# Down projection: the last three wide matmuls of one stretch alternate with the first four narrow ones of the next, at two places

## The chip, the cores and the metric

One core of a Trainium2 chip runs the whole program in one launch. The metric is device time in microseconds (us). The kernel before took 2168.19 us as the median of three runs (2166.08 to 2170.76). Engines go by these names: PE (TensorE, matmuls) with its weight loads PEld, DVE (VectorE), ACT (ScalarE), POOL (GpSimd) and SP (SyncE, which only issues DMAs here).

## What is computed

One decoder block, float32, 512 tokens, model width 2048: modulated RMS norm, a combined input projection, two token mixers, an output projection, and then the gated MLP on which this case turns:

```python
D_MODEL = 2048; SEQ = 512; D_FF = ((8 * D_MODEL // 3 + 255) // 256) * 256     # 5632 = 44 * 128

def _conv_ffn(h, w_up, conv_w, conv_b, w_down):
    u = h @ w_up                                   # (512, 2 * 5632)
    y = conv_b + causal depthwise conv of width 3 over u
    val, gate = jnp.split(y, 2, axis=-1)
    return (jax.nn.silu(gate) * val) @ w_down      # (512, 5632) @ (5632, 2048)

x = x + gt2 * _conv_ffn(...)
return _rmsnorm(x, norm_f_g)
```

## The kernel before

Activations lie transposed: 128 features on the partitions, the 512 tokens along the free dimension. Each float32 product is made of three matmuls of rounded halves: the weight tile is split into a high part `wh` and a rest `wl`, the activation into `xh` and `xl`, and `mm3` (L131) issues `wh*xh`, `wh*xl` and `wl*xh` (L133, L134, L135) into one PSUM bank. ACT makes the high part (L1373) and DVE the rest (L1374), both in `wsplit`, into one of three rotating buffers that the profile names `uw`. So a 128x128 weight tile costs three matmuls, each with a weight load of its own. A matmul streams either all 512 tokens (here called wide) or a half of 256 (narrow).

The down projection has 44 blocks of 128 input features and 16 output tiles `f`, and is done in this order on PE:

1. `plain(A1, 0)`: 4 input blocks against all 16 output tiles, wide. Each tile's partial sum is copied out by ACT (L1675) and written to DRAM (`yd`, L1676) by POOL's queue. The profile names its operands `act`.
2. `strassen`: 16 input blocks by a scheme of seven products for eight over the two halves of tokens, of output tiles and of inputs. Eight rounds of seven products, 24 narrow matmuls each; the operands are named `Y` and `T`. Results are added to `yd` in DRAM by POOL's queue (L1688, L1731). In the last round `rest_pair` loads the activations of the remaining blocks (L1500).
3. `down_four` and the loop over `f` up to 7: the 20 remaining blocks (`A3`), wide, 60 matmuls for a tile. `load_x2` fetches the residual `x2` and the stored `yd` of a tile (POOL's queue, L1821) and adds them (DVE, L1822); `last_residual` adds the tile's PSUM (DVE, L1250), sums squares for the norm (ACT L1241, DVE L1242) and scales. `gate_row` (DVE, L1789) works out the gates beside it.
4. `down_half(0, f)` for `f` = 8 to 15: the same for the first half of the tokens, narrow, 60 matmuls for a tile; then the same for the second half, and the final norm.

The order of each engine's instructions is set by a scheduling layer that simulates the program; `tc.issue_after` ties an instruction behind another. Small tiles of 512 columns (`Slot`) come from a list of about ten homes in strict rotation: `yd` in `load_x2` takes one, and so does `sqx` in `last_residual`; a new user waits until the last user of that home is done. DVE, ACT and the queues work in order.

Of the kernel before, what the change touches and what calls it, by code (L numbers as in the profile page):

```python
# [17 lines left out]
T = 512  # L18
D = 2048
KT = D // P  # L20
# [6 lines left out]
NWF = 8  # L27
# [40 lines left out]
def block_kernel(ctx, tc, a, out, stop=None, dbg=None):  # L68
    nc = tc.nc
    V, S, G, PE = nc.vector, nc.scalar, nc.gpsimd, nc.tensor  # L70
# [26 lines left out]
    def col(name, i):  # L97
        return vec[:, COLS[name] + i : COLS[name] + i + 1]
# [29 lines left out]
        eng.tensor_tensor(lo, raw, hi[:, :].bitcast(F32), op=ALU.subtract)  # L128
        return hi, lo

    def mm3(ps, wh, wl, xh, xl, start, stop, more=False):  # L131

        PE.matmul(ps, wh, xh, start=start, stop=False, skip_group_check=more)  # L133
        PE.matmul(ps, wh, xl, start=False, stop=False, skip_group_check=more)  # L134
        return PE.matmul(ps, wl, xh, start=False, stop=stop, skip_group_check=more)  # L135

    def project(ps, src, acts, start=True, stop=True, engs=(V,)):

# [50 lines left out]
    blocks = []  # L189
# [1005 lines left out]
    def bank():  # L1195
        return psm.tile([P, T], F32, tag="b", name="b")

    def half(acts, hf):
        sl = slice(hf * HT, (hf + 1) * HT)
        return [t[:, :, sl] for t in acts]  # L1200
# [5 lines left out]
    def wide(name):  # L1206

        return rb.tile([P, 4, HT], F32, tag="wide", name=name, bufs=3)
# [8 lines left out]
    def x2(f, sl=slice(0, T)):  # L1217
        return x2q[f // 4][:, f % 4, sl]
# [27 lines left out]
    def residual(f, pss, gate, acc, lo, hi, fresh):  # L1246

        x = x2(f, slice(lo, hi))
        for ps in pss:
            V.scalar_tensor_tensor(x, ps, gate, x, op0=ALU.mult, op1=ALU.add)  # L1250
        sumsq(acc, x, lo, hi, fresh)
# [115 lines left out]
    def wsplit(src, off=0):  # L1367
        n = src.shape[-1]
        i = nsplit[0] % 3
        nsplit[0] += 1  # L1370
        w = (ea, ea, ub)[i].tile([P, WS], F32R, tag=f"w{i}", name="uw")
        hi, lo = w[:, off : off + n], w[:, 2 * QW + off : 2 * QW + off + n]
        S.copy(hi, src)  # L1373
        lo_of[0] = V.tensor_tensor(lo, src, hi.bitcast(F32), op=ALU.subtract)  # L1374
        return hi, lo

    def product(ps, w, Y, start=True):
        wh, wl = wsplit(w, 16)
        n = w.shape[-1] // P
        for k in range(n):  # L1380
            sl = slice(k * P, (k + 1) * P)
            y = Y[k // 4]
            mm3(ps, wh[:, sl], wl[:, sl], y[:, 0, k % 4, :], y[:, 1, k % 4, :], start=start and k == 0,
                stop=k == n - 1, more=not start)
# [95 lines left out]
    NR = NF - 3 * ND  # L1480
# [84 lines left out]
    def last_operands(name):  # L1565
        for h in held:
            if h[0] != name:
                continue
            if len(h) == 4:
                make(name, h[1], pairwise(h[2]), 2, h[3])  # L1570
                h[2].done()
            else:
                make(*h)

    A1, A3 = [], []
# [9 lines left out]
    def last_product(p):  # L1585

        j, u1, u2, b, w22, x = p
        product(b, w22, T4, start=False)
        if x is None:
            S.copy(u2[:, H0], b)  # L1590
        else:
            V.tensor_add(u2[:, H0], x[:, H0], b)
            x.done()
        finish_pair(j, u1, u2)
# [64 lines left out]
    yd = [tc.dram_tile([P, T], F32, name=f"yd{f}") for f in range(KT)]  # L1659

    def plain(acts, k0):

        nk = len(acts)
        for f in range(KT):
            w = wide("wd").rearrange("p a b -> p (a b)")
            nc.sync.dma_start(w, a["wdn"][f, :, k0 * P : (k0 + nk) * P])
            wh, wl = wsplit(w, 0)
            ps = bank()
            for k in range(nk):
                sl = slice(k * P, (k + 1) * P)  # L1670
                mm3(ps, wh[:, sl], wl[:, sl], acts[k][:, 0, :], acts[k][:, 1, :], start=k == 0, stop=k == nk - 1)
            if f == 0:
                last_product(pend)
            s_ = Slot("yd")
            S.copy(s_.t, ps)  # L1675
            G.dma_start(yd[f], s_.t)  # L1676
            s_.done()
            for _ in range(2 if f else 1):
                next(prep, None)
        for _ in prep:  # L1680
            pass

    def last_down(p):

        f, u2, b, w22 = p
        product(b, w22, ops["T4"], start=False)
        S.activation(u2[:, H0], b, AF.Copy, scale=-1.0)
        G.dma_start(yd[f], u2.t, accum_op=ALU.add)  # L1688
        u2.done()

    def strassen(hook):

        wq = [rb.tile([P, 4 * QW], F32, tag=f"x2_{i}", name="wd4") for i in (0, 2, 1, 3)]
        pend = None
        for f in range(NWF):
            wa, wb = wq[2 * (f % 2)], wq[2 * (f % 2) + 1]
            w11, w12, w21, w22 = (t[:, s_] for t in (wa, wb) for s_ in (W1, W2))
            nc.sync.dma_start(wa, a["wdn"][f, :, ND * P : 3 * ND * P])
            nc.sync.dma_start(wb, a["wdn"][f + NWF, :, ND * P : 3 * ND * P])
            pa = bank()[:, 0:HT]  # L1700
            cap = Slot("cap")
            product(pa, w11, ops["Y11"])
            S.copy(cap[:, H0], pa)
            if pend:
                last_down(pend)
            u1 = Slot("u1")
            pb = bank()[:, 0:HT]
            product(pb, w12, ops["Y21"])
            V.tensor_add(u1[:, H0], cap[:, H0], pb)
            hook(f, 0)  # L1710
            u2 = Slot("u2")
            pc = bank()[:, 0:HT]
            r1 = wide("r1").rearrange("p a b -> p (a b)")
            V.tensor_add(r1, w21, w22)
            product(pc, r1, ops["T1"])
            S.copy(cap[:, H1], pc)
            if f == 0:
                last_operands("T3")
            hook(f, 1)
            r2 = wide("r2").rearrange("p a b -> p (a b)")  # L1720
            V.tensor_add(r2, r1, w11)
            product(pa, r2, ops["T2"], start=False)
            S.copy(cap[:, H0], pa)
            if f == 0:
                last_operands("T4")
            hook(f, 2)
            r4 = wide("r4").rearrange("p a b -> p (a b)")
            V.tensor_add(r4, r2, w12)
            product(pc, r4, ops["Y22"], start=False)
            V.tensor_add(u1[:, H1], cap[:, H0], pc)  # L1730
            G.dma_start(yd[f], u1.t, accum_op=ALU.add)  # L1731
            u1.done()
            hook(f, 3)
            r3 = wide("r3").rearrange("p a b -> p (a b)")
            V.tensor_add(r3, w11, w21)
            product(pa, r3, ops["T3"], start=False)
            V.scalar_tensor_tensor(u2[:, H1], pa, -1.0, cap[:, H1], op0=ALU.mult, op1=ALU.subtract)
            cap.done()
            pend = (f + NWF, u2, pa, w22)
        return pend  # L1740
# [5 lines left out]
    def in_last(f, i):  # L1746
        if f == NWF - 1:
            rest_pair(G)

    plain(A1, 0)  # L1750
    pend = strassen(in_last)

    wd2 = ea.tile([P, 2, 2 * QW], F32, tag="t41", name="wd2")
# [2 lines left out]
    def down_row():  # L1756
        if nrow[0] % 5 > 2:
            w = wd2[:, nrow[0] % 5 - 3, :]
        else:
            w = wide("wd").rearrange("p a b -> p (a b)")  # L1760
        nrow[0] += 1
        return w

    def down(ps, f, acts, blocks=(0, 8, 16)):
        for k0 in blocks:
            n = min(8, NR - k0)
            w = down_row()
            nc.sync.dma_start(w[:, 0 : n * P], a["wdn"][f, :, (3 * ND + k0) * P : (3 * ND + k0 + n) * P])
            wh, wl = wsplit(w[:, 0 : n * P], 16 if acts[0].shape[-1] == HT else 0)
            for k in range(n):  # L1770
                sl = slice(k * P, (k + 1) * P)
                x = acts[k0 + k]
                mm3(ps, wh[:, sl], wl[:, sl], x[:, 0, :], x[:, 1, :], start=k0 + k == 0, stop=k0 + k == NR - 1)

    cb = []

# [36 lines left out]
    def gate(f):  # L1813
        return mod[:, 80 + f : 81 + f]
# [12 lines left out]
    def down_half(hf, f):  # L1827
        ps = bank()[:, 0:HT]
        down(ps, f, half(A3, hf))
        last_residual(f, [ps], hf * HT, (hf + 1) * HT)  # L1830

    def last_residual(f, ps, lo, hi):
        residual(f, ps, gate(f), acc, lo, hi, f == 0)
        S.activation(x2(f, slice(lo, hi)), x2(f, slice(lo, hi)), AF.Identity, bias=eps[:, 2:3], scale=col("nf", f))
# [6 lines left out]
    for f in range(NWF):  # L1841
        if f == 0:
            pss = down_four()
        if f >= 4:
            gate_row()
        load_x2(f)
        ps = pss[f] if f < 4 else bank()
        if f >= 4:
            down(ps, f, A3)
            gate_row()  # L1850
        last_residual(f, [ps], 0, T)
    for f in range(NWF, KT):
        if gated[0] < KT and f % 2 == 0:
            gate_row()
# [111 lines left out]
```

## Time and profile before

| | us |
|---|---|
| median of the three runs | 2168.19 |
| the profiled execution's own time | 2164.5 |
| its span, first to last instruction | 2162.7 |
| DVE busy | 1677.9 |
| ACT busy | 1046.7 |
| POOL busy | 236.2 |
| down projection, from the first wide `act` matmul to the end | 1668 to 2163 |

The mean granted PE clock was 0.991. Section 1 of the page gives busy time as a share of the span, section 4 the chain of work that ended last. The timeline view has a row for each instruction with start, duration, engine, line, operands and shape; in square brackets stands the idle time before it and who ended that. PE's durations overlap, since matmuls are pipelined: the pace of PE is read from the starts, or from the number of matmuls in a stretch (the windows view, "x1106").

### The profile page before, as it was taken

What the parts mean: (1) busy time and instruction counts of PE and PEld (TensorE: products, weight loads), DVE (VectorE), ACT (ScalarE), POOL (GpSimd) and SP (SyncE); (2) the same over time, 40 slices, a digit from 0 to 9 for tenths busy, and PEclk for the clock granted to TensorE, in tenths of its full rate; (3) what the DMA queues carried; (4) which work ended last, traced back from release to release, by engine and by line L of the source; (5) the groups of instructions that cost most, each with busy time, mean ns of one, the idle gap of its engine ahead of it and who ended that gap; (6) DMA issues with size and microseconds to landing.
All of it is one profiled execution on the core that took longest, in us unless ns stands there. A gap on an engine that the chain in (4) does not pass through costs nothing.

```text
span 2162.7 us, 44015 instructions
## 1 busy us (share of the span) xinstructions
PE 2118.8 (98%) x17864; PEld 1874.0 (87%) x17864; DVE 1677.9 (78%) x2615; ACT 1046.7 (48%) x1510; POOL 236.2 (11%) x376
## 2 busy tenths in 40 slices
PE   8999999999999999999999999999999999999997
PEld 3567777777767889999999999999999899987897
DVE  7988898888854677888888877887778557768664
ACT  4354444443433466655555555555556444443353
POOL 0002122222100111101100100000000000120000
PEclk9999999999999999999999999999999999999998
DMA  9966665656437565988989877777777535598754
GB/s 393 405 220 197 199 203 170 204 172 185 145 111 269 184 197 186 289 252 250 244 250 260 223 212 209 209 207 206 207 211 226 196 124 138 143 334 307 240 184 165
DMA packets 169485, 471.89 MB, mean 218 GB/s; under 512 B 21361, under 2 KB 29505, under 8 KB 159169
## 3 DMA queue, kind: packets, MB, share of 16 engines
q1 hardware_dynamic: 120370, 352.12, 47.8%
q0 software_dynamic: 27696, 79.20, 17.5%
q10 hardware_dynamic: 21216, 37.76, 5.7%
q8 instruction: 140, 2.29, 0.4%
q14 instruction: 63, 0.52, 0.1%
HBM read 432.81 MB, written 36.18 MB: 217 GB/s over the span
## 4 chain that ended last, share of the span: by engine, by line
PE 87%; DMA 4%; DVE 4%; ACT 2%; issue 2%; POOL 0%; DVEq 0%; SPq 0%; ACTq 0%; POOLq 0%
PE b L135 19%; PE b L133 19%; PE b L134 19%; PE mm L631 11%; PE pf L412 4%; PE b L1203 2%; PE b L1204 1%; DMA wrow<-wup 1%; PE pb L1033 1%; DVE war L750 1%; DMA wraw<-wout 1%; DMA wa<-ada 1%; PE pa L697 0%; ACT x L1303 0%; PE pf L133 0%
## 5 line engine op out<-in xcount | busy, mean ns | idle before, releaser
L135 PE MATMUL b<-t,uw 128*128 128x256 f32 x1408 | 388.6, 276 | 0.0
L133 PE MATMUL b<-t,uw 128*128 128x256 f32 x1408 | 388.6, 276 | 0.0
L134 PE MATMUL b<-t,uw 128*128 128x256 f32 x1408 | 388.6, 276 | 0.0
L133 PE MATMUL b<-y,uw 128*128 128x256 f32 x1056 | 293.7, 278 | 2.9 <-ACT uw L1373 2.9
L135 PE MATMUL b<-y,uw 128*128 128x256 f32 x1056 | 292.9, 278 | 0.8 <-DVE uw L1374 0.7
L134 PE MATMUL b<-y,uw 128*128 128x256 f32 x1056 | 292.9, 277 | 0.0
L631 PE MATMUL mm<-ahl,whi 128*128 128x512 f32 x864 | 290.5, 410 | 2.0 <-DVE rk L534 1.4
L133 PEld LDWEIGHTS b<-t,uw 128*128 128x128 f32 x1408 | 264.3, 188 | 0.0
L134 PEld LDWEIGHTS b<-t,uw 128*128 128x128 f32 x1408 | 264.3, 188 | 0.0
L135 PEld LDWEIGHTS b<-t,uw 128*128 128x128 f32 x1408 | 264.3, 188 | 0.0
L1374 DVE TENSOR_TENSOR uw<-r,uw 128x1024 fp32r<-128x1024 f32 x164 | 200.4, 1223 | 79.1 <-ACT uw L1373 79.1
L1374 DVE TENSOR_TENSOR uw<-wquart,uw 128x1024 fp32r<-128x1024 f32 x156 | 190.7, 1223 | 68.0 <-ACT uw L1373 67.7
L1373 ACT CAST uw<-wquart 128x1024 fp32r<-128x1024 f32 x156 | 164.0, 1052 | 89.1 <-PE b L135 66.1
L1374 DVE TENSOR_TENSOR uw<-wd,uw 128x1024 fp32r<-128x1024 f32 (+1 forms) x112 | 123.9, 1108 | 105.6 <-ACT uw L1373 105.3
L135 PE MATMUL b<-act,uw 128*128 128x256 f32 (+1 forms) x608 | 202.2, 333 | 2.6 <-DVE uw L1374 2.6
L133 PEld LDWEIGHTS b<-y,uw 128*128 128x128 f32 x1056 | 199.7, 189 | 3.6 <-ACT uw L1373 3.5
L133 PE MATMUL b<-act,uw 128*128 128x256 f32 (+1 forms) x608 | 202.3, 333 | 0.0
L1373 ACT CAST uw<-r 128x1024 fp32r<-128x1024 f32 x164 | 172.5, 1052 | 61.5 <-PE b L135 61.5
L134 PE MATMUL b<-act,uw 128*128 128x256 f32 (+1 forms) x608 | 202.1, 332 | 0.0
L135 PEld LDWEIGHTS b<-y,uw 128*128 128x128 f32 x1056 | 199.7, 189 | 1.2 <-DVE uw L1374 1.2
L134 PEld LDWEIGHTS b<-y,uw 128*128 128x128 f32 x1056 | 199.7, 189 | 0.1
L631 PEld LDWEIGHTS mm<-ahl,whi 128*128 128x128 f32 x864 | 158.6, 189 | 43.3 <-issue 12.2
(356 smaller groups left out, 4600.9 us busy)
## 6 DMA issues: line engine op xcount, KB each, us to landing
wquart<-wup SPq DMA_DIRECT2D x176, 512.0 KB, 5.3
wa<-ada SPq DMA_DIRECT2D x48, 1024.0 KB, 9.5
war<-ada SPq DMA_DIRECT2D x192, 256.0 KB, 4.0
wd<-wdn SPq DMA_DIRECT2D x64, 512.0 KB, 4.4
wraw<-win ACTq DMA_DIRECT2D x118, 256.0 KB, 4.2
wraw<-wout SPq DMA_DIRECT2D x96, 256.0 KB, 3.5
wquart<-wup POOLq DMA_DIRECT2D x44, 512.0 KB, 6.8
r<-wup SPq DMA_DIRECT2D x44, 512.0 KB, 4.6
```

The source lines that it names most:

```text
L133: PE.matmul(ps, wh, xh, start=start, stop=False, skip_group_check=more)
L134: PE.matmul(ps, wh, xl, start=False, stop=False, skip_group_check=more)
L135: return PE.matmul(ps, wl, xh, start=False, stop=stop, skip_group_check=more)
L412: PE.matmul(pf[n % 2 * 4 + ii], w[:, sl], full[k], start=k == 0, stop=k == KT - 1)
L631: PE.matmul(ps, w[:, sl], x, start=first, stop=k == KT - 1 and i == 2)
L750: V.scalar_tensor_tensor(wa, wa, 1.0, cqs[kq], op0=ALU.mult, op1=ALU.mult, accum_out=modq[:, kq, j : j + 1])
L1033: PE.matmul(pt[HS[e], h, c * 2 * L : (c + 1) * 2 * L], nt[HS[e], s, :], rw[HS[e], s, :, :], start=True, stop=True)
L1203: PE.matmul(ps[:, :].rearrange("p (a b) -> p a b", a=2), wh, x, start=start, stop=False)
L1204: PE.matmul(ps[:, 0:HT], wl, x[:, 0, :], start=False, stop=stop)
L1373: S.copy(hi, src)
L1374: lo_of[0] = V.tensor_tensor(lo, src, hi.bitcast(F32), op=ALU.subtract)
```

## The change

Place 1 is the passage from `plain` to `strassen`, place 2 the passage from tile 7 to `down_half(0, 8)`. There `mm3` holds back the last three wide matmuls (`hold`), and the next call of `mm3`, which is the first of the narrow ones, issues its own first matmul, then one held back, its second, one held back, its third, and the last held back; the fourth narrow one follows. No matmul is added or taken away. What comes after the held sum moves behind the first narrow tile's code: `stored(15, ps)` (the copy of the last `plain` tile) behind the first product of `strassen`, `last_residual(7, ...)` behind the matmuls of `down_half(0, 8)`.

```diff
+    late = []
+    def mm3(ps, wh, wl, xh, xl, start, stop, more=False, hold=False):
+        muls = [lambda: PE.matmul(ps, wh, xh, ...), lambda: PE.matmul(ps, wh, xl, ...), lambda: PE.matmul(ps, wl, xh, ...)]
+        if hold:
+            late.extend(muls)
+            return None
+        if late:
+            ins = muls[0]()
+            for m in (late.pop(0), muls[1], late.pop(0), muls[2], late.pop(0)):
+                with tc.issue_after(ins.ins):
+                    ins = m()
+            return ins
...
@@ plain
-                mm3(ps, wh[:, sl], wl[:, sl], acts[k][:, 0, :], acts[k][:, 1, :], start=k == 0, stop=k == nk - 1)
+                mm3(ps, wh[:, sl], wl[:, sl], acts[k][:, 0, :], acts[k][:, 1, :], start=k == 0, stop=k == nk - 1,
+                    hold=f == KT - 1 and k == nk - 1)
...
+        return lambda: stored(KT - 1, ps)
@@ strassen
             product(pa, w11, ops["Y11"])
+            if f == 0:
+                finish_plain()
@@ down_half
         down(ps, f, half(A3, hf))
+        if f == NWF and hf == 0:
+            last_residual(NWF - 1, [held_ps], 0, T)
         last_residual(f, [ps], hf * HT, (hf + 1) * HT)
@@ the loop over wide tiles
-            down(ps, f, A3)
+            down(ps, f, A3, hold=f == NWF - 1)
...
-        last_residual(f, [ps], 0, T)
+        if f < NWF - 1:
+            last_residual(f, [ps], 0, T)
+    held_ps = ps
```

PE at place 1, before: the last wide matmuls of `plain` (operand `act_19145`) and the first narrow ones of `strassen` (`Y_19323`).

```order
L133 MATMUL b<-act_19145,uw 128x512
L134 MATMUL b<-act_19145,uw 128x512
L135 MATMUL b<-act_19145,uw 128x512
L133 MATMUL b<-Y_19323,uw 128x256
L134 MATMUL b<-Y_19323,uw 128x256
L135 MATMUL b<-Y_19323,uw 128x256
L133 MATMUL b<-Y_19323,uw 128x256
```

The same place in the changed kernel (its L135, L136 and L137 are the three matmuls of `mm3`):

```order
L135 MATMUL b<-Y_19323,uw 128x256
L135 MATMUL b<-act_19145,uw 128x512
L136 MATMUL b<-Y_19323,uw 128x256
L136 MATMUL b<-act_19145,uw 128x512
L137 MATMUL b<-Y_19323,uw 128x256
L137 MATMUL b<-act_19145,uw 128x512
L135 MATMUL b<-Y_19323,uw 128x256
```

Each of the last three wide matmuls now has a narrow one on either side; the rows ahead and behind are as they were. Place 2 is changed in the same way.

POOL's queue near place 2, before: the loads of `yd` for `load_x2` of tiles 7 to 15.

```order
L1821 DMA yd_22278<-yd7_19189 128x512
L1821 DMA yd_22370<-yd8_19190 128x512
L1821 DMA yd_22454<-yd9_19191 128x512
L1821 DMA yd_22539<-yd10_19192 128x512
L1821 DMA yd_22624<-yd11_19193 128x512
L1821 DMA yd_22709<-yd12_19194 128x512
L1821 DMA yd_22793<-yd13_19195 128x512
L1821 DMA yd_22877<-yd14_19196 128x512
L1821 DMA yd_22960<-yd15_19197 128x512
```

And in the changed kernel:

```order
L1844 DMA yd_22278<-yd7_19189 128x512
L1844 DMA yd_22454<-yd9_19191 128x512
L1844 DMA yd_22362<-yd8_19190 128x512
L1844 DMA yd_22539<-yd10_19192 128x512
L1844 DMA yd_22624<-yd11_19193 128x512
L1844 DMA yd_22709<-yd12_19194 128x512
L1844 DMA yd_22877<-yd14_19196 128x512
L1844 DMA yd_22960<-yd15_19197 128x512
L1844 DMA yd_22793<-yd13_19195 128x512
```

The load for tile 13 went from before 14 and 15 to behind them, since the rotation of the `Slot` homes is shifted by one: it now takes the home that `sqx` of tile 7 had, and waits for DVE's add of that tile (`acc`, before L1242); before, it took the home of `yd` of tile 8.

DVE at the same place, before: from the add of `yd` of tile 13 (L1822) to the weight rest of the second block of tile 9 (`uw_22488`).

```order
L1822 SCALAR_TENSOR_TENSOR x2_21565<-yd_22793,mod_87,x2_21565 128x512
L1374 TENSOR_TENSOR uw_22404<-wd_22402,uw_22404 128x1024
L1250 SCALAR_TENSOR_TENSOR x2_21563<-b_22281,mod_87,x2_21563 128x512
L1374 TENSOR_TENSOR uw_22433<-wd_22431,uw_22433 128x512
L1242 TENSOR_TENSOR acc_21566<-acc_21566,sqx_22361 128x512
L1374 TENSOR_TENSOR uw_22460<-wd_22458,uw_22460 128x1024
L1374 TENSOR_TENSOR uw_22488<-wd2_21561,uw_22488 128x1024
```

And in the changed kernel:

```order
L1388 TENSOR_TENSOR uw_22399<-wd_22397,uw_22399 128x1024
L1264 SCALAR_TENSOR_TENSOR x2_21563<-b_22281,mod_87,x2_21563 128x512
L1388 TENSOR_TENSOR uw_22428<-wd_22426,uw_22428 128x512
L1256 TENSOR_TENSOR acc_21566<-acc_21566,sqx_22444 128x512
L1388 TENSOR_TENSOR uw_22460<-wd_22458,uw_22460 128x1024
L1845 SCALAR_TENSOR_TENSOR x2_21565<-yd_22793,mod_87,x2_21565 128x512
L1388 TENSOR_TENSOR uw_22488<-wd2_21561,uw_22488 128x1024
```

The add of `yd` of tile 13 now stands five rows later, between two weight rests of tile 9, behind the `acc` of tile 7 that its load waits for.

More of the change, by code (lines that the diff above doesn't have):

```diff
@@ L129, in split_weights @@
         return hi, lo
[L131 to L135, printed above, removed]
+    late = []
+    def mm3(ps, wh, wl, xh, xl, start, stop, more=False, hold=False):
+        muls = [lambda: PE.matmul(ps, wh, xh, start=start, stop=False, skip_group_check=more),
+                lambda: PE.matmul(ps, wh, xl, start=False, stop=False, skip_group_check=more),
+                lambda: PE.matmul(ps, wl, xh, start=False, stop=stop, skip_group_check=more)]
+        if hold:
[7 more added lines that the diff above has]
+            return ins
+        for m in muls:
+            ins = m()
+        return ins
     def project(ps, src, acts, start=True, stop=True, engs=(V,)):
@@ L1670, in plain @@
                 sl = slice(k * P, (k + 1) * P)
-                mm3(ps, wh[:, sl], wl[:, sl], acts[k][:, 0, :], acts[k][:, 1, :], start=k == 0, stop=k == nk - 1)
+                mm3(ps, wh[:, sl], wl[:, sl], acts[k][:, 0, :], acts[k][:, 1, :], start=k == 0, stop=k == nk - 1,
+                    hold=f == KT - 1 and k == nk - 1)
             if f == 0:
                 last_product(pend)
[L1674 to L1677, printed above, removed]
+            if f < KT - 1:
+                stored(f, ps)
             for _ in range(2 if f else 1):
@@ L1681, in plain, with stored @@
             pass
+        return lambda: stored(KT - 1, ps)
+    def stored(f, ps):
+        s_ = Slot("yd")
+        S.copy(s_.t, ps)
+        G.dma_start(yd[f], s_.t)
+        s_.done()
     def last_down(p):
@@ L1748, in in_last @@
             rest_pair(G)
-    plain(A1, 0)
+    finish_plain = plain(A1, 0)
     pend = strassen(in_last)
@@ L1762, in down_row, with down @@
         return w
-    def down(ps, f, acts, blocks=(0, 8, 16)):
+    def down(ps, f, acts, blocks=(0, 8, 16), hold=False):
         for k0 in blocks:
@@ L1772, in down @@
                 x = acts[k0 + k]
-                mm3(ps, wh[:, sl], wl[:, sl], x[:, 0, :], x[:, 1, :], start=k0 + k == 0, stop=k0 + k == NR - 1)
+                mm3(ps, wh[:, sl], wl[:, sl], x[:, 0, :], x[:, 1, :], start=k0 + k == 0, stop=k0 + k == NR - 1,
+                    hold=hold and k0 + k == NR - 1)
     cb = []
```

## The prediction

> **What bounds the kernel now.** I read the page first, section 1 and the chain:
>
> ```profile
> PE 2118.8 (98%) x17864; PEld 1874.0 (87%) x17864; DVE 1677.9 (78%) x2615; ACT 1046.7 (48%) x1510; POOL 236.2 (11%) x376
> PE 87%; DMA 4%; DVE 4%; ACT 2%; issue 2%; POOL 0%; DVEq 0%; SPq 0%; ACTq 0%; POOLq 0%
> ```
>
> PE is always busy and makes up the chain. No work is removed, so only PE's pace can give anything, and a matmul's duration does not show pace. So next the number of matmuls in stretches where PE runs one kind without a gap (the windows view: stretch, length, PE's busy time and number, granted clock, DMA share and rate):
>
> ```profile
> 900.00:1660.00 760.00, 760.00 (x6709) 1.00 0.82 226
> 1760.00:1890.00 130.00, 130.00 (x1106) 1.00 0.54 154
> 2036.00:2096.00 60.00, 60.00 (x512) 1.00 0.57 186
> 2107.00:2145.00 38.00, 38.00 (x338) 1.00 0.57 193
> ```
>
> All four are narrow matmuls of one shape at one granted clock. Adding 0.28 us, since a matmul that only reaches into the stretch counts, 760.28/6709 is 113.3 ns from start to start in the up projection, 130.28/1106 is 117.8 in `strassen`, 60.28/512 is 117.7 in the first-half tiles, and 38.28/338 is 113.3 in the second-half ones, which read the same tiles as the first. So the narrow stream has two paces, 4.44 ns apart, and keeps either for hundreds of matmuls: a state, not a cost of the tiles. How the slow one begins, from the timeline at place 1 and place 2:
>
> ```profile
> 1758.50 0.39 PE L135 MATMUL b<-act,uw 128*128 128x512 f32 x1
> 1758.73 0.28 PE L133 MATMUL b<-Y,uw 128*128 128x256 f32 x1
> 1758.84 0.28 PE L134 MATMUL b<-Y,uw 128*128 128x256 f32 x1
> ...
> 2033.27 0.39 PE L135 MATMUL b<-act,uw 128*128 128x512 f32 x1
> 2033.50 0.28 PE L133 MATMUL b<-act,uw 128*128 128x256 f32 x1
> ```
>
> No gap: wide ones start 0.23 apart, and the narrow ones are at 0.118 from the first. These are the two places that the change touches.
>
> **The change, part by part.** *The alternation itself.* The output projection alternates wide and narrow. How it begins, after a run of wide ones, and how one such stretch ends in narrow ones:
>
> ```profile
> 730.51 0.39 PE L1203 MATMUL b<-ahl,whi 128*128 128x512 f32 x1
> 730.74 0.28 PE L1204 MATMUL b<-ahl,wlo 128*128 128x256 f32 x1
> ...
> 731.21 0.40 PE L1203 MATMUL b<-ahl,whi 128*128 128x512 f32 x1
> 731.45 0.28 PE L1204 MATMUL b<-ahl,wlo 128*128 128x256 f32 x1
> 731.57 0.40 PE L1203 MATMUL b<-ahl,whi 128*128 128x512 f32 x1
> 731.80 0.28 PE L1204 MATMUL b<-ahl,wlo 128*128 128x256 f32 x1
> ...
> 823.99 0.39 PE L1203 MATMUL b<-ahl,whi 128*128 128x512 f32 x1
> 824.22 0.28 PE L1204 MATMUL b<-ahl,wlo 128*128 128x256 f32 x1
> 824.34 0.28 PE L134 MATMUL b<-y,uw 128*128 128x256 f32 x1
> ...
> 824.57 0.28 PE L133 MATMUL b<-y,uw 128*128 128x256 f32 x1
> ...
> 825.02 0.28 PE L134 MATMUL b<-y,uw 128*128 128x256 f32 x1
> ```
>
> From the narrow one at 730.74 to the fourth at 731.80 are 1.06 us for three of each. Plain order takes three times 0.227 and three times 0.118, 1.03. So a place costs 0.03, two of them 0.06 us, and the last wide one is later by 0.37 us: at place 2 the first narrow one takes the start of the first held one, 2 x 0.23 ahead of 2033.27, and the last wide one starts 1.06 - 0.23 = 0.83 behind that, at 2033.64.
>
> *The pace behind it.* This is where the gain is, if any. The trace has no case of just this order, so both ends: 0, if the pace stays 117.8, and 113.3 for the whole stretch. The nearest row for the second is the end of alternation above: from 824.57 to the fourth narrow one behind it, 825.02, are 0.45 us, so 113, where the slow pace would take 0.47. I take the fast end for both places, on that one case; but it is one. At place 1 the stretch runs from 1759 until PE's pace stops mattering, which is in the last round of `strassen`:
>
> ```profile
> 1896.28 1.08 POOL L1500 DMA_DIRECT2D act<-ad  x2 [0.27 <-PE b L135]
> ...
> 1903.84 6.97 DMA act<-ad
> ```
>
> POOL's loads wait for PE to leave a tile at 1896.28; from there loads, casts and POOL's queue lead to the two waits of PE at 1906 and 1911 with latencies of their own, which would only move along. So 137 us / 117.8 = 1163 matmuls at 4.44 ns, 5.2 us. At place 2 it runs to 2097, where the statistics of the norm interrupt PE: 63.1 us / 117.7 = 536, 2.4 us. Beyond it the pace is what the interruption leaves, as before.
>
> *The load for tile 13.* It now waits for tile 7's `acc`, and DVE's add of it stands ahead of `uw_22488`. Rows of before (timeline of DVE, POOL and PE, then landing times of these `yd` loads from 1990 to 2020, and of all `yd` DMAs):
>
> ```profile
> 2012.86 0.75 DVE L1822 SCALAR_TENSOR_TENSOR x<-yd,mod,x 128x512 f32<-128x512 f32 x1
> 2013.90 0.55 POOL L1821 DMA_DIRECT2D yd<-yd  x1 [11.19 <-DVE mod L1790]
> 2035.15 0.69 DVE L1242 TENSOR_TENSOR acc<-acc,sqx 128x512 f32<-128x512 f32 x1
> 2040.43 1.23 DVE L1374 TENSOR_TENSOR uw<-wd,uw 128x1024 fp32r<-128x1024 f32 x1 [1.60 <-ACT uw L1373]
> 2043.63 0.28 PE L135 MATMUL b<-act,uw 128*128 128x256 f32 x1
> 2045.12 1.22 DVE L1374 TENSOR_TENSOR uw<-wd,uw 128x1024 fp32r<-128x1024 f32 x1
> 2047.87 0.28 PE L135 MATMUL b<-act,uw 128*128 128x256 f32 x1
> DMA to landing us min/median/max: 5.4/6.1/6.7
> DMA to landing us min/median/max: 2.3/4.2/9.4
> ```
>
> `acc` ends at 2035.15 + 0.69 + 0.37 = 2036.2, POOL issues 0.29 later (13.90 against 13.61), 2036.5. With a landing of L the add starts at 2036.55 + L, `uw_22488` 0.67 behind it, and is ready 1.23 later: 2038.45 + L. PE wants it at 2043.66 (43.63 + 0.03), at the fast pace 0.37 earlier. DVE then has a dense row of work until the next block's rest, 5.9 us from the start of `uw_22488` to 2046.34 before, which PE wants at 2047.90, or 2047.4 at the fast pace. So PE loses L - 4.8 at the slow pace, L - 4.3 at the fast. Ends: nothing at 2.3, 4.6 or 5.1 at 9.4. I take 5.4, the low end of the loads nearest in time, because the DMA engines are less busy here:
>
> ```profile
> 2007.00:2014.00 7.00, 7.00 (x32) 5.80 (x31) 7.00 (x11) 2.63 (x4) 0.10 (x1) 1.00 0.82 259
> 2035.00:2042.00 7.00, 7.00 (x62) 7.00 (x61) 3.53 (x6) 3.65 (x5) 0.00 (x0) 1.00 0.53 173
> ```
>
> The last two columns are share and rate: 0.53 against 0.82. That is 1.1 us at the fast pace. Such a wait can also change the pace; after the one at 1906 it became fast:
>
> ```profile
> 1906.81 0.39 PE L135 MATMUL b<-T,uw 128*128 128x256 f32 x1 [0.70 <-DVE uw L1374]
> ...
> 1907.51 0.28 PE L134 MATMUL b<-T,uw 128*128 128x256 f32 x1
> 1907.62 0.28 PE L135 MATMUL b<-T,uw 128*128 128x256 f32 x1
> ```
>
> so I cost that at nothing if the pace is fast already.
>
> *Edits with no price.* The weights of the first narrow tile are wanted 0.7 us earlier, three wide starts. DVE's rests for them are ready at 1750.84 and 2028.42:
>
> ```profile
> 1749.61 1.23 DVE L1374 TENSOR_TENSOR uw<-wd,uw 128x1024 fp32r<-128x1024 f32 x1 [2.96 <-ACT uw L1373]
> ...
> 2027.20 1.22 DVE L1374 TENSOR_TENSOR uw<-wd,uw 128x1024 fp32r<-128x1024 f32 x1
> ```
>
> 7.9 and 5.1 us ahead of 1758.73 and 2033.50. The copy of the last `plain` tile is late by as much as that tile's last matmul, 0.37 us, on an ACT that is 48% busy. Wide matmuls ahead of the places and ACT's idle time hide these; were that cover gone, each would show as its own few tenths.
>
> **The sum.** -5.2 - 2.4 + 0.06 + 1.1 = -6.4 us: from 2164.5, the profiled execution's own time, to 2158.1. That execution lies 3.7 below the median of the runs, so against 2168.19 it is 2161.8.
>
> **The rivals.** *The pace stays slow.* For it: after three pairs the alternation at 730 is where it began within the view's 0.01 us (0.23 into 731.80 as into 730.74, with 0.24 between), so three pairs may leave no trace; and the end at 824 came soon after a wait of PE. Against it: that end, and that the pace is a state which small shifts can flip. Then only 0.06 and the late load remain, 0.6 at L = 5.4 (the slow pace); if that wait flips the rest of the first-half tiles, some 415 matmuls, it gives back 1.8. So 2167 to 2169. The Trainium skill, "TensorE: Matmul & The Clock Gate", section "Back-to-back issue gap", gives the spacing of warm matmuls as a function of their columns alone (N/2.4 + 2.5 ns; my estimate from it for 256 is 109). By that rule order is free and the time stays at 2168.2; the two paces of one shape in this trace speak against the rule; its chance lies within that of this rival.
>
> *Only one place flips.* Place 1 alone: -5.2 + 0.06 + 0.6 = -4.5, 2163.7. Place 2 alone: -2.4 + 1.2 = -1.2, 2167.0.
>
> *Slower: the load of tile 13.* At the slow pace it decides from L = 4.8 on, and costs more than 4.3 us from 9.1; with the 9.4 of the slowest `yd` DMA it would be 4.7, 2172.9. Against it: no load of this line near here took over 6.7.
>
> **How the numbers follow.** 0.2% (4.3 us) is about what a measurement of this kernel can tell from no change. Both places fast 0.47, place 1 alone 0.07: both beyond it, though place 1 alone barely, so 0.51 for faster. Slow pace 0.34 and place 2 alone 0.06, with the remaining 0.03: 0.43 for the same. Late load or a pace worse than either 0.06: slower. Range: from 2159.5 (no late load, less the scatter of the runs) to 2169.5 (slow pace, with its wait). The likeliest case by itself spans 2159.5 to 2163.5.
>
> **What will show it.** Right: 1760 to 1885 holds about 1105 narrow matmuls instead of 1063 (125.28 us by either pace), 2050 to 2090 about 355 instead of 342; a new wait of PE for DVE near 2043 to 2048. Wrong: starts 118 ns apart behind both places. I would be wrong by the most if place 1 stays slow, and otherwise if faster narrow matmuls uncover a new wait in `strassen`'s first round.

## The result, and the profile after

The changed kernel took 2159.92 us as the median of 14 executions (2155.93 to 2165.58), the kernel before 2169.02 on the same chip (14 executions, 2164.10 to 2197.17). The ratio is 0.9956, 95% interval 0.994 to 0.9972: faster, by less than half a per cent. On the 2168.19 of the first section that is 2158.7 us, 0.8 below the lower end of the predicted range and 3.1 below the predicted time. Executions of every kernel here fall on two levels 30 us apart, for a cause that experiments 7 and 8 show; two of the 14 of before lie on the upper one, none of the changed kernel's.

The page after, section 1 and the chain:

```profile
PE 2110.9 (98%) x17864; PEld 1866.0 (86%) x17864; DVE 1678.0 (78%) x2615; ACT 1047.8 (48%) x1510; POOL 237.0 (11%) x376
PE 86%; DMA 5%; DVE 4%; ACT 2%; issue 2%; POOL 1%; POOLq 0%; ACTq 0%; DVEq 0%; SPq 0%
```

PE has as many matmuls as before and is busy 7.9 us less; it is still the bound. The stretches of one kind (windows view: stretch, length, PE's busy time and number of matmuls, granted clock, DMA share and rate), in order the up projection, `strassen`, and the first-half tiles twice:

```profile
900.00:1660.00 760.00, 760.00 (x6708) 1.00 0.82 226
1770.00:1900.00 130.00, 130.00 (x1149) 1.00 0.55 153
2036.00:2094.00 58.00, 58.00 (x515) 1.00 0.62 201
...
2050.00:2090.00 40.00, 40.00 (x355) 1.00 0.62 198
```

In 130 us of `strassen` there are 1149 narrow matmuls where there were 1106: 130.28/1149 = 113.4 ns. In the first-half tiles it is 58.28/515 = 113.2, and 2050 to 2090 holds the predicted 355. This execution reached `strassen` 5 us later than the one before, so the prediction's first stretch is 1765 to 1890 here, and holds the predicted 1105 too. The up projection has its pace of before. How the fast pace begins at place 1 (timeline):

```profile
1763.30 0.39 PE L136 MATMUL b<-act,uw 128*128 128x512 f32 x1
1763.53 0.39 PE L137 MATMUL b<-act,uw 128*128 128x512 f32 x1
1763.75 0.28 PE L135 MATMUL b<-Y,uw 128*128 128x256 f32 x1
1763.87 0.40 PE L135 MATMUL b<-act,uw 128*128 128x512 f32 x1
1764.10 0.28 PE L136 MATMUL b<-Y,uw 128*128 128x256 f32 x1
1764.22 0.39 PE L136 MATMUL b<-act,uw 128*128 128x512 f32 x1
1764.45 0.28 PE L137 MATMUL b<-Y,uw 128*128 128x256 f32 x1
1764.57 0.39 PE L137 MATMUL b<-act,uw 128*128 128x512 f32 x1
1764.80 0.28 PE L135 MATMUL b<-Y,uw 128*128 128x256 f32 x1
1764.91 0.28 PE L136 MATMUL b<-Y,uw 128*128 128x256 f32 x1
1765.03 0.28 PE L137 MATMUL b<-Y,uw 128*128 128x256 f32 x1
1765.14 0.28 PE L135 MATMUL b<-Y,uw 128*128 128x256 f32 x1
1765.25 0.28 PE L136 MATMUL b<-Y,uw 128*128 128x256 f32 x1
```

Three pairs from 1763.75 to 1764.80 are 1.05 us, and from the fourth narrow matmul on the starts are 0.113 apart. The late load of tile 13's `yd` (timeline of DVE and POOL, then what the tile view gives for it):

```profile
2036.25 0.69 DVE L1256 TENSOR_TENSOR acc<-acc,sqx 128x512 f32<-128x512 f32 x1
2037.24 0.55 POOL L1844 DMA_DIRECT2D yd<-yd  x1 [22.05 <-DVE acc L1256]
...
2041.29 0.75 DVE L1845 SCALAR_TENSOR_TENSOR x<-yd,mod,x 128x512 f32<-128x512 f32 x1 [1.79 <-DMA yd<-yd]
2041.95 1.22 DVE L1388 TENSOR_TENSOR uw<-wd,uw 128x1024 fp32r<-128x1024 f32 x1
DMA to landing us min/median/max: 4.0/4.0/4.0
```

It does wait for `acc`, as worked out, and DVE waits 1.79 us for it. But it lands 4.0 us after its issue, and the rest (`uw`) that stands behind it is ready at 2043.17, ahead of PE's use; PE has no wait from 2035 to 2060.

The two spans, 2162.7 and 2160.9 us, differ by only 1.8, because this execution reached the first wide matmul of the down projection 5.6 us later, in code that is alike. The first row is of before, the second of after (timeline):

```profile
1668.27 0.40 PE L133 MATMUL b<-act,uw 128*128 128x512 f32 x1
...
1673.88 0.40 PE L135 MATMUL b<-act,uw 128*128 128x512 f32 x1
```

From there to the end are 494.4 us before and 487.0 after: 7.4 us less.

### The profile page after: what moved, and what is told of

Its sections match the earlier page's. It is cut to its first block, busy times and chain, and to the rows that moved or that the text cites. A ratio compares the mean times of both kernels' runs of the same rounds, so it can differ in the third digit from the quotient of the medians.

```text
span 2160.9 us, 44013 instructions
## 1 busy us (share of the span) xinstructions
PE 2110.9 (98%) x17864; PEld 1866.0 (86%) x17864; DVE 1678.0 (78%) x2615; ACT 1047.8 (48%) x1510; POOL 237.0 (11%) x376
## 4 chain that ended last, share of the span: by engine, by line
PE 86%; DMA 5%; DVE 4%; ACT 2%; issue 2%; POOL 1%; POOLq 0%; ACTq 0%; DVEq 0%; SPq 0%
PE b L137 19%; PE b L135 19%; PE b L136 19%; PE mm L645 11%; PE pf L426 4%; PE b L1217 2%; PE b L1218 1%; DMA wrow<-wup 1%; PE pb L1047 1%; DVE war L764 1%; DMA wraw<-wout 1%; DMA wa<-ada 1%; PE pa L711 0%; ACT x L1317 0%; DMA wraw<-win 0%
## 5 line engine op out<-in xcount | busy, mean ns | idle before, releaser
L137 PE MATMUL b<-t,uw 128*128 128x256 f32 x1408 | 388.6, 276 | 0.0
L135 PE MATMUL b<-t,uw 128*128 128x256 f32 x1408 | 388.6, 276 | 0.0
L136 PE MATMUL b<-t,uw 128*128 128x256 f32 x1408 | 388.6, 276 | 0.0
L135 PE MATMUL b<-y,uw 128*128 128x256 f32 x1056 | 293.6, 278 | 4.1 <-ACT uw L1387 4.1
L137 PE MATMUL b<-y,uw 128*128 128x256 f32 x1056 | 292.8, 278 | 0.8 <-DVE uw L1388 0.7
L136 PE MATMUL b<-y,uw 128*128 128x256 f32 x1056 | 292.9, 277 | 0.0
L135 PEld LDWEIGHTS b<-t,uw 128*128 128x128 f32 x1408 | 264.3, 188 | 0.0
L136 PEld LDWEIGHTS b<-t,uw 128*128 128x128 f32 x1408 | 264.3, 188 | 0.0
L137 PEld LDWEIGHTS b<-t,uw 128*128 128x128 f32 x1408 | 264.3, 188 | 0.0
L135 PEld LDWEIGHTS b<-y,uw 128*128 128x128 f32 x1056 | 199.5, 189 | 4.8 <-ACT uw L1387 4.8
L137 PE MATMUL b<-act,uw 128*128 128x256 f32 (+1 forms) x608 | 200.5, 330 | 2.7 <-DVE uw L1388 2.7
L135 PE MATMUL b<-act,uw 128*128 128x256 f32 (+1 forms) x608 | 200.7, 330 | 0.0
L137 PEld LDWEIGHTS b<-y,uw 128*128 128x128 f32 x1056 | 199.5, 189 | 1.2 <-DVE uw L1388 1.2
L136 PE MATMUL b<-act,uw 128*128 128x256 f32 (+1 forms) x608 | 200.4, 330 | 0.0
L136 PEld LDWEIGHTS b<-y,uw 128*128 128x128 f32 x1056 | 199.6, 189 | 0.1
```

The lines of the kernel that those rows point to most:

```text
L135: muls = [lambda: PE.matmul(ps, wh, xh, start=start, stop=False, skip_group_check=more), lambda: PE.matmul(ps, wh, xl, start=False, stop=F ...
L136: lambda: PE.matmul(ps, wh, xl, start=False, stop=False, skip_group_check=more),
L137: lambda: PE.matmul(ps, wl, xh, start=False, stop=stop, skip_group_check=more)]
```

## The experiments

Theory: the alternation takes PE's narrow stream into its fast pace, and the gain is the number of narrow matmuls behind each place times 4.44 ns. Rivals: the gain comes from what was moved on the other engines; the pace is drawn by chance; a part of the 9 us has another cause.

Where a mean is given for one of the two levels, it says so ("below 2180"). All the means of before are of 101 executions on the chips of all experiments: 71 below 2180, mean 2166.97, and 30 above, mean 2196.8.

**1. Place 1 alone.** Place 2 and the order of the `yd` loads as before the change:

```
-            down(ps, f, A3, hold=f == NWF - 1)
+            down(ps, f, A3)
...
-        if f < NWF - 1:
-            last_residual(f, [ps], 0, T)
+        last_residual(f, [ps], 0, T)
```

> Only place 1 alternates; tile 7 and the first-half tiles are written as before the change, and the loads of yd are in their old order. Theory (the alternation sets the pace of the narrow matmuls behind it): strassen at 113.3 ns from its fourth narrow matmul on, so about 1105 narrow ones in a 125.28 us stretch of it; first-half tiles at 117.7 as before. From the first narrow matmul at place 1 to the end of strassen's last wait 149 us instead of 154, so -4.8 us, ratio 0.9978. Rival 1 (the gain comes from what else was moved, or from the code's new place in the program): this stage gains nothing, or gains together with the stretch behind place 2. Rival 2 (the pace is drawn anew at each execution): any mix of paces, without regard to where the order was changed.

The windows, the first one the up projection, the second `strassen`, the third the first-half tiles:

```profile
900.00:1660.00 760.00, 760.00 (x6455) 1.00 0.79 218
1795.00:1925.00 130.00, 130.00 (x1149) 1.00 0.55 153
2060.00:2118.00 58.00, 58.00 (x495) 1.00 0.58 183
```

`strassen` is fast (113.4 ns), the first-half tiles slow (58.28/495 = 117.7). The ratio, 0.9989 with an interval from 0.9956 to 1.0021, decides nothing: three of ten executions were on the upper level. The other seven have a mean of 2160.6, 6.4 ± 1.6 below before (95%, as with each ± here), where the theory had 4.8. The profiled one took 2189.87 us, and the first row shows why: its up projection ran at 760.28/6455 = 117.8 ns.

**2. Place 2 alone**; `plain` without the held mm3:

```
-            if f < KT - 1:
-                stored(f, ps)
+            stored(f, ps)
...
-            if f == 0:
-                finish_plain()
```

> Only place 2 alternates (with tile 7's residual behind down_half(0, 8) and the new order of the yd loads); place 1 as before the change. Theory: strassen at 117.8 ns (1249 of its matmuls), first-half tiles at 113.3 until the statistics at about 2096; -2.4 us there, ratio 0.9989. The late load of tile 13 lands within about 4 us of its issue and PE doesn't wait for it. Rival 1 (side effects): gain elsewhere, or none here. Rival 3 (the late load does cost the 1.1 us of the prediction): a wait of PE for DVE between 2040 and 2050, and the gain is 1.3.

```profile
1765.00:1895.00 130.00, 130.00 (x1106) 1.00 0.53 149
2036.00:2094.00 58.00, 58.00 (x514) 1.00 0.62 202
```

Slow in `strassen`, fast in the first-half tiles: each place sets only the stretch behind it. The ratio, 1.0029 (0.9992 to 1.0066), is again of both levels; the eight executions below 2180 have a mean of 2164.2, 2.8 ± 1.6 below before, where the theory had 2.4. The late load landed in 3.8 us, and PE didn't wait.

**3. All the moves, but PE's order of before.**

```
-            ins = muls[0]()
-            for m in (late.pop(0), muls[1], late.pop(0), muls[2], late.pop(0)):
+            ins = late.pop(0)()
+            for m in (late.pop(0), late.pop(0), *muls):
```

> All that the change moves on ACT, DVE, POOL and SP stays moved, but the three held wide matmuls are issued first, then the narrow ones: PE's instructions stand in exactly the order of before. Theory: both stretches at 117.8 and 117.7 ns, span within 1 us of before, ratio 1.000. Rival 1 (what was moved on the other engines brings the gain, or part of it): some or all of the 0.44% stays, ratio 0.9956 to 0.998.

```profile
1765.00:1895.00 130.00, 130.00 (x1106) 1.00 0.53 149
2038.00:2096.00 58.00, 58.00 (x495) 1.00 0.59 188
```

Both slow, ratio 1.0005 (0.9995 to 1.0015). What was moved on the other engines brings nothing; PE's order brings all. This bears on the rule that the prediction weighs, the Trainium skill's "TensorE: Matmul & The Clock Gate", section "Back-to-back issue gap". That section gives its formula for an isolated matmul and says that in a stream of weight loads and matmuls both set the spacing, which the prediction leaves out. Neither has the order of the matmuls in it, and here one order gives 117.8 ns and another 113.4 for the same instructions.

**4. One pair in place of three**, W W N W N N (W wide, N narrow):

```
-            ins = muls[0]()
-            for m in (late.pop(0), muls[1], late.pop(0), muls[2], late.pop(0)):
+            ins = late.pop(0)()
+            for m in (late.pop(0), muls[0], late.pop(0), muls[1], muls[2]):
```

> As the changed kernel, but only one pair changes places at each of the two places: wide, wide, narrow, wide, narrow, narrow. Theory A (one narrow matmul in front of a wide one is enough to set the pace): both stretches at 113.3 ns, ratio 0.9956 as with three pairs. Theory B (it takes several pairs, as the run of alternation in the output projection had): both stretches stay at 117.8 and 117.7, ratio 1.000. I lean to A at 0.55.

```profile
1765.00:1895.00 130.00, 130.00 (x1149) 1.00 0.55 155
2035.00:2093.00 58.00, 58.00 (x514) 1.00 0.61 197
```

Fast at both places: theory A. One narrow matmul ahead of the last wide one does it. The ratio, 1.0006 (0.9958 to 1.0054), is of six executions above 2180 and six below; experiment 10 has more.

**5. What sets the pace.** Matmuls added ahead of products of `strassen`, with other data and a result that the product then overwrites (one execution, the profiled one):

```
+    COLS_OF = dict(W=2 * HT, N=HT, H=HT // 2)
...
+        for c in kinds:
+            n = COLS_OF[c]
+            rhs = Y[0][:, 0, 0:2, :].rearrange("p a b -> p (a b)")[:, 0:n]
+            ins = PE.matmul(full[:, 0:n], wh[:, 0:P], rhs, start=True, stop=True)
```

> Place 1 in plain order (as before), and in strassen 32 added matmuls whose results are overwritten, ahead of the first narrow matmul of some products, to see what sets the pace of the narrow ones behind them. W is 512 columns, N 256, H 128. Round 0: second product W, third WWW. Round 1: WNW, none, WWW. Round 2: WWNW, none, WWW. Round 3: H, H, WWW. Round 4: HH, WW, WWW. Round 5: WNWNWNW, none, W. Round 6: WNW, WNW, H. Round 7: WWW. At place 2 the three held wide ones follow the first narrow one in a row: N, W, W, W, N, N. Theory A (what counts is how many wide ones stand right in front of the narrow ones: one gives the fast pace, two or more the slow): fast (113 ns) behind W, WNW, WWNW and WNWNWNW, slow (118) behind WW and WWW, slow at place 2; H and HH change nothing or shift the state once. Theory B (the state flips at each lone wide one, whatever it was): W takes slow to fast and fast to slow, so the second WNW of round 6 doesn't keep what the first gave. Theory C (only the alternation that the change writes, with both streams' real operands, does it): slow throughout.

Four of its stretches, behind the WWW of round 0, the WNW of round 1, the WWW of round 1 and the W of round 5:

```profile
1797.50:1807.50 10.00, 10.00 (x87) 1.00 0.45 173
1809.50:1816.50 7.00, 7.00 (x62) 1.00 0.58 171
1818.50:1828.50 10.00, 10.00 (x91) 1.00 0.33 96
1902.00:1911.00 9.00, 9.00 (x82) 1.00 0.49 143
```

10.28/87 is 118 ns, 7.28/62 is 117, 10.28/91 is 113 and 9.28/82 is 113. Theory C falls, since added matmuls flip the pace too. Theory A falls: WWW led to fast in two of six cases. What fits is that WWW changes the pace, from whichever it was to the other (four times fast to slow, twice slow to fast), W likewise (twice slow to fast), and WW keeps fast. WNW led to slow from either (three cases), WWNW took fast to slow, WNWNWNW kept slow. A lone H changed the pace in its three cases, and HH took slow to fast. Place 2, N W W W N N, was fast. So the number of wide ones counts, and theory B has half of it.

**6. Two pairs and four**, as a test of that count on the change itself: the same function with two pairs at place 1 (one held matmul is issued first) and four at place 2 (two mm3 held):

```
-                    hold=hold and k0 + k == NR - 1)
+                    hold=hold and k0 + k >= NR - 2)
```

> As the changed kernel, but two pairs at place 1 (W W N W N W N N) and four at place 2 (W N W N W N W N N), W 512 columns, N 256. Theory (each lone wide matmul between narrow ones flips the pace, so the number of pairs decides: odd is fast, even slow; from e5: one wide fast, WNW slow, WNWNWNW slow, and three pairs in the changed kernel fast): strassen 118 ns, first-half tiles 118 ns, 7.4 us of gain gone, ratio about 1.000. Rival (any alternation of both sizes with real operands gives the fast pace, and the added matmuls of e5 behaved otherwise because they wrote one bank): both 113 ns, ratio 0.996.

```profile
1795.00:1925.00 130.00, 130.00 (x1106) 1.00 0.52 145
2067.00:2125.00 58.00, 58.00 (x494) 1.00 0.59 188
```

Both slow, ratio 0.9989 (0.9946 to 1.0031). Real operands and alternation alone aren't enough: one pair and three are fast, two and four slow. The change would have brought nothing with two pairs; of four, only place 2 was run.

**7 and 8. The up projection made fast, and made slow.** The changed kernel with WNW added at about 891 us, and in 7 a W one product later:

```
+            product(pa, w11, Y11, kinds="WNW" if n == 0 else "", full=fa)
...
+            product(pb, w12, Y21, kinds="W" if n == 0 else "", full=fb)
```

> The changed kernel with four added matmuls in the up projection (results overwritten): WNW ahead of the first product of its second loop (about 891 us), which in e5 led to the slow pace from either state, and one W ahead of the second product, which led from slow to fast. Theory (the 30 us by which some executions of every kernel here are longer are the up projection, some 7000 narrow matmuls at 118 in place of 113 ns): the up projection is fast in every execution from there on, cost of the four 0.8 us, all runs near 2161 and none near 2190. Rival (the two levels of total time come from something else, and the pace in the profiled executions only coincided): about one run in four still near 2190.

> As e7, but only the WNW, which by e5 leads to the slow pace from either state. Theory: some 6800 narrow matmuls of the up projection at 118 ns in every execution, 30.2 us, all runs near 2191. Rival: runs near 2161 as well.

The up projection in 7 and in 8:

```profile
900.00:1660.00 760.00, 760.00 (x6709) 1.00 0.81 225
...
900.00:1660.00 760.00, 760.00 (x6455) 1.00 0.78 218
```

With W behind WNW all 12 executions lie between 2158.0 and 2163.5 us (median 2161.8, ratio 0.9953, interval 0.992 to 0.9985). With WNW alone all 10 lie between 2185.2 and 2191.7 (median 2189.5, ratio 1.0068, 1.0027 to 1.011). So the two levels are the pace of the up projection: 254 matmuls fewer in 760 us. The difference of the medians, 27.8 us, is 2.4 less than the 30.2 expected. In the two profiled executions the up projection itself differs by 30.3 us (from the first narrow matmul behind WNW to the first wide one of the down projection, 781.0 and 811.3), and the down projection by 3.2 the other way, as PE's waits at the end of `strassen` were longer in 7; whether that holds for the other executions isn't settled. The cost of the four added ones was taken as 0.8 us; 7 has a mean 2.0 above the changed kernel's executions below 2180. But the changed kernel itself also falls on the upper level (experiment 10). Over all executions the mean of 7 is 2161.4, against 2162.2 for the 32 of the changed kernel, a difference well within their scatter, and 2175.8 for the 101 of before.

**9. The changed kernel again**, unchanged, for the size of the gain.

> The changed kernel once more, for the size of its gain over before among executions whose up projection is fast: 7.4 us by the two traces, 9.5 by the first comparison. Theory (the first comparison was high by scatter): the median of the runs below 2180 lies 6 to 8 us under that of before, and the profiled run has no wait of PE between 2035 and 2060. Rival (something of 2 us beyond the pace was gained, which the one trace happens not to show): 9 us or more.

2157.61 us, median of six (ratio 0.9893, 0.9832 to 0.9954, of which most is that 10 of the 29 executions of before beside it were on the upper level). All six were below 2180; their mean is 8.8 below that of before on this chip, 2166.9. The profiled one has both stretches fast (1149 and 514 matmuls in the same windows), a landing of 3.8 us, and no wait of PE. By itself this lies between theory and rival, with a scatter of ± 2.7 that reaches both; the mean over all executions in experiment 10 speaks for the theory.

**10. The changed kernel and the one-pair kernel, once more on one chip.**

> The changed kernel for the third time, beside the one-pair kernel and the kernel before on one chip: of 20 executions of it so far none was above 2180 us, of 88 of the kernel before 21, of 12 of the one-pair kernel 6, though all issue the same instructions up to the end of the up projection. Theory (the up projection's pace is drawn by the waits ahead of it, alike for all; the 20 were chance or a matter of the chip): about one in four above 2180 here too. Rival (something in the changed program keeps the up projection fast): none above 2180, while before and the one-pair kernel have them. In both cases the median of those below 2180 is 6 to 8 us under before's.

> The one-pair kernel again. Both theories: executions on both levels, a quarter to a half above 2180 us; those below within 1 us of the changed kernel's in the median, since one pair and three give the same pace behind them.

The changed kernel: 2160.99 us, ratio 0.9934 (0.9892 to 0.9976), three of twelve above 2180. One pair: 2159.56, ratio 0.9947 (0.9911 to 0.9982), one of twelve above. The rival falls: the changed program does not keep the up projection fast. (Up to then 22 of 78 executions of before were above 2180, not the 21 of 88 of the expectation.) Whether the changed kernel is above less often stays open: 3 of 32 executions, against 30 of 101 of before and 7 of 24 of the one-pair kernel, whose code is alike up to there. One of twelve is also less than the quarter expected for one pair. Over all executions below 2180, the changed kernel's mean (29) is 7.6 ± 1.25 us under that of before (71), and one pair's (17) 7.2 ± 1.2.

**11. More added patterns.**

> As e5, with other added matmuls ahead of the first, second and third product of each round of strassen: round 0: none, WW, W; round 1: W, W, WNW; round 2: N, W, N; round 3: WNW, W, HH; round 4: WNW, W, WWWW; round 5: WNW, WWWW, WNW; round 6: WNNW, WNW, W; round 7: WNNW. Place 2: N W W N W N N behind the run of wide ones. Theory (an odd row of wide ones flips the pace from either state, an even one keeps it, WNW leads to slow from either state, as e5 had it): round 0 slow, slow, fast; round 1 slow, fast, slow; round 2 slow, fast, fast; round 3 slow, fast, open; round 4 slow, fast, fast; round 5 all slow; round 6 open, slow, fast; place 2 fast. Rival (a row of wide ones leads to one pace for each length, whatever the state before: one and two to fast, three to slow unless the pace had been slow): WW takes slow to fast in round 0, and the first W of round 1 keeps fast.

This too is one execution. Of the twenty entries that the theory filled 17 came out, the first W of round 1 (fast to slow) and WW and WWWW (kept the pace) among them, so the rival falls. Of the open ones HH kept fast, and WNNW kept slow in round 6 and fast in round 7. What didn't come out: the W of round 2, one product and 48 narrow matmuls behind a lone added N, left the pace slow (and so it still was behind the next N), and place 2 (N W W N W N N) was slow. The windows of these two:

```profile
1805.00:1817.00 12.00, 12.00 (x105) 1.00 0.41 111
2046.00:2096.00 50.00, 50.00 (x427) 1.00 0.58 187
```

12.28/105 is 117 ns, 50.28/427 is 117.7. So the count of wide ones is most of the rule and not all of it: one narrow matmul more ahead of the W seems to matter too, by these two cases. The rest of the rule stays open.

## Why the prediction was right, and where it was wrong

**The mechanism was right.** Both places went fast and nothing else brought time (experiments 1 to 3). The ground for it was thin: one case, the end of the output projection's alternation. Two pairs would have been as near to that case, and are slow (experiment 6). That the change had three was luck, as far as the prediction goes: nothing in it tells three pairs from two.

**Place 1: -5.2 predicted, -4.8 in the traces.** 1245 matmuls at 4.44 ns are 5.5 us; then the waits in the last round of `strassen` were 0.75 longer in this execution. The second row of each pair below is the later wait (before, then after):

```profile
1911.78 0.39 PE L133 MATMUL b<-Y,uw 128*128 128x256 f32 x1 [2.18 <-ACT cap L1716]
...
1908.04 0.38 PE L137 MATMUL b<-T,uw 128*128 128x256 f32 x1 [1.75 <-DVE uw L1388]
1912.70 0.38 PE L135 MATMUL b<-Y,uw 128*128 128x256 f32 x1 [1.88 <-ACT cap L1738]
```

2.88 us with the 0.70 at 1906.81 before, 3.63 after. The loads behind those waits do not follow PE's pace, as predicted, and the waits scatter. From the twentieth wide matmul ahead of place 1 to the twentieth ahead of place 2 are 267.0 to 271.2 us in the eight traces with `strassen` fast (after, experiments 1, 4, 7 to 10) and 272.8 to 274.8 in the four with it slow (before, 2, 3, 6). The means, 268.9 and 273.9, are 5.0 apart.

**Place 2: -2.4 predicted, -2.4 in the traces** (about 535 matmuls until the statistics, as worked out). From the twentieth wide matmul ahead of place 2 to the statistics are 65.75 to 65.76 us in the eight traces of these twelve that are fast there, and 68.13 to 68.15 in the four slow ones.

**The alternation: +0.06 predicted;** 0.02 to 0.03 a place by the rows.

**The late load: +1.1 predicted, 0 measured.** This is the step that failed: a term of the sum that was sized too large. Its path was right (the load waits for `acc`, the rest stands behind its add, PE would lose what L exceeds 4.3 at the fast pace), but L was taken as 5.4, from loads at a DMA share of 0.82. It was 4.0 in the changed kernel and 3.7 to 4.0 in the nine other traces with this load (experiments 2 to 4 and 6 to 10): always below the 4.3. Among the slow traces, the stretch to the statistics took 68.13 and 68.15 us with the late load (experiments 3 and 6) and 68.13 with the old order (before and experiment 1), and none of the twelve traces has a gap in PE's starts there, so PE lost nothing by it. The prediction's 0.53 for the share is from before, where no load of `yd` runs there. The same window after:

```profile
2035.00:2042.00 7.00, 7.00 (x64) 7.00 (x64) 3.78 (x6) 4.60 (x6) 0.55 (x1) 1.00 0.75 226
```

The share was 0.75 with the load in it, between the two. So the group of loads nearest in time was the wrong one to size L by, its low end too; the prediction's other row, the median of 4.2 over all `yd` DMAs, would have given nothing for the term.

**A lower clock behind waits** was not in the sum, and came out near nothing. Windows of before (first two) and after (last two), behind the last waits of `strassen` and behind those of the next stage:

```profile
1904.00:1922.00 18.00, 15.12 (x108) 13.96 (x108) 13.14 (x18) 9.37 (x14) 5.83 (x11) 1.00 1.00 338
1975.00:1982.00 7.00, 4.63 (x14) 3.37 (x14) 7.00 (x8) 2.84 (x5) 0.55 (x1) 0.79 0.81 284
...
1906.00:1924.00 18.00, 14.36 (x92) 13.25 (x90) 12.45 (x16) 8.52 (x13) 5.25 (x10) 0.91 0.99 365
1977.00:1984.00 7.00, 4.63 (x21) 3.52 (x20) 7.00 (x9) 3.19 (x5) 1.10 (x2) 1.00 0.88 296
```

The third column from the end is the granted clock. Before it fell in the second window (0.79), after in the first (0.91). Of 7 us at 0.79 and 18 at 0.91, 1.5 and 1.6 us are lost, so the two nearly cancel.

**The sum and the range.** Without the late load the sum is -7.5 us; the two traces show -7.4 from the first wide matmul of the down projection on, and the executions below 2180 show -7.6 ± 1.25. So nearly all of the sum's error is the one term. It alone does not put the time outside the range, whose lower end, 2159.5, is the sum without the term (2160.7) less 1.2 us for the scatter of the runs. The first comparison's 9.5 us lie above the 7.6 by more than that; with 14 executions on each side its interval reaches from 6.1 to 13.0. A part of this may be the two executions of before on the upper level: among those below 2180 alone, 12 and 14, the difference of the means is 8.0 ± 2.2, which from 2168.19 would be 2160.2, inside the range. The three runs that the prediction had to go by all lie on the lower level.

## What to carry to other kernels

Where PE is the bound, count matmuls in equal windows along the whole kernel, not their durations' sum: one kind of stream can run at two paces 4% apart, and a few matmuls at its head, or a wait, decide which. A pace that was entered by chance is worth setting on purpose at the head of the longest stretch, and testing there with one matmul more and one less, since what flips it mostly flips it back (a lone added wide one flipped it in eight of nine cases, from either pace). And before a comparison of a few per mille is read, look whether the executions fall on levels, and compare within one level.

## What the runs showed of the hardware that was not expected

The pace of a long stream can differ from one execution to the next where waits precede it. Behind its last waits, near 870 us, the up projection's 7000 narrow matmuls took 113.3 ns in most profiled executions and 117.8 in others (experiments 1, 5 and 6), of programs that are alike up to there; and 30 of 101 executions of the kernel before were 30 us longer. At the passages from wide to narrow without a wait, each order gave the same pace in every profiled execution.

A matmul's duration does show its pace, other than the prediction says. Groups by line in `strassen` before, and after (count, busy us, mean ns):

```profile
L133 PE MATMUL b<-T,uw 128*128 128x256 f32 x208 | 58.4, 281 | 0.0
...
L135 PE MATMUL b<-T,uw 128*128 128x256 f32 x223 | 61.5, 276 | 0.0
```

281 ns at the slow pace, 276 at the fast. And the state is kept over thousands of matmuls, but a single one of 512 columns (eight of nine cases) or of 128 (three of three) turns it over: in experiment 5 one H took fast to slow and another slow to fast. What holds it, no run here shows.
